# One encoder block on one core: loads of the attention stage a block ahead, the merge of the dilated groups in pinned steps, and gate stores on ScalarE's queue

## The chip, the cores and the metric

The kernel runs on one core of one Trainium2 chip. The metric is the device time of one execution in microseconds (us). The kernel before has a median of 1679.76 us over three runs.

## The reference, cut to what matters

The block takes 1024 tokens of width 1024, all in fp32. One projection of the normalised input gives q, k and v for two token mixers and two gates; both mixers are attention, over different sets of keys.

```python
a = rms_norm(h, g_mix[i])
qa, ka, va, qd, kd, vd, gate_na, gate_dil = jnp.split(a @ w_in[i], split_points, axis=-1)
y_na = merge(neighborhood_attention(heads(qa, 8), heads(ka, 8), heads(va, 8), rpb[i]))
y_dil = merge(dilated_attention(rotary(heads(qd, 12), positions), rotary(heads(kd, 12), positions), heads(vd, 12)))
mixed = sigmoid(gate_na) * (y_na @ w_branch_na[i]) + sigmoid(gate_dil) * (y_dil @ w_branch_dil[i])
h = h + mixed @ w_out[i]
h = h + square(relu(rms_norm(h, g_mlp[i]) @ w_up[i])) @ w_down[i]
h = h + sigmoid(rms_norm(h, g_ple[i]) @ w_ple_gate[i]) * (p[i] @ w_ple_proj[i])
...
def dilated_attention(q, k, v):                # three groups of four heads: (window, dilation)
...
    w = jax.nn.softmax(jnp.stack(lses), axis=0)         # the groups are merged per head slot
    return jnp.einsum('gbhs,gbhsd->bhsd', w, jnp.stack(outs))
```

Neighbourhood attention has eight heads on a 16x64 grid of tokens, with a window of 8x16 and a bias per head.

## The kernel before, in words

**Precision and products.** Every fp32 operand is split into a high and a low part ("hi" and "lo"): ScalarE casts (`split`, L107), VectorE or GpSimd subtracts (L108). A product is three matmuls (hi·hi, lo·hi, hi·lo), a score product two.

**Stages.** The products of the extra input, the v projection and the q, k projection (ten units of seven products, `unit`) come first; q and k go to a DRAM buffer `qk_scr`, v to `v_scr`. Then comes the stage of this change, from about 363 us to 742 us of the span:

- **Gates.** Sixteen pieces of gate weights (`w_in` from number 10) are multiplied with the activations. `gates` (L573 to 588) is a generator; each of its 256 steps is three matmuls of 512 columns. `take` and `prep` (L132 to 144) load a piece (`w_raw`, two buffers, 512 KB), cast it and subtract. The first 24 steps (`FILL_HEAD`) are written ahead of the attention, the others are filled between its tiles, 1.5 steps per dilated tile and 1.35 per neighbourhood tile. A result is copied by ScalarE (L586) and stored to `g_scr` on SyncE's queue (L587), 32 stores.
- **Dilated attention.** Twelve heads (numbers 8 to 19) of eight tiles of 128 queries; heads are served in pairs `pr`. Per head `load_raw` loads q and k, and `operands` (L600 to 613) makes the operands: ScalarE writes `q_st` and `k_st` (L607, L608), VectorE finishes `q_st` (L610), GpSimd makes `k_lo` (L611). Per tile: scores on TensorE, row minimum on VectorE (`nm`, L628), exponent on ScalarE (L630), transposes on TensorE, split, product with v (`av`), and the result added up in `numer`.
- **Neighbourhood attention.** Eight heads (0 to 7), for each four column blocks `cb` of two tiles `qt`. `na_score` loads v (four DMAs) and the bias (L667), which GpSimd negates (L668), and after the exponent VectorE takes a reciprocal (`rs`, L680) and GpSimd normalises the row (`s_sb`, L681). `na_turn` transposes (L691), `na_av` multiplies with v (L713, L714), and VectorE adds up `y_na` (L726).
- **Merge of the dilated groups.** `dil_stats` stores minima and sums of a group, `dil_merge` computes the weights after head 1, and `dil_out(0)`, `dil_out(1)` after heads 3 and 5 scale and add the three groups (L913 to L916; products and sums of 128x1024 on VectorE) into `y_d`.
- **Branches.** Six tiles of `y` are loaded back from `y_scr` (`y_raw`, L972, two buffers), split into `y_op`, and multiplied with the branch weights (`ps_b`); the sigmoids of the gates multiply the result (L989).

**What sets the order.** TensorE's instructions keep the order in which the program writes them (`pe`): scores run three tiles ahead of the transposes (`AHEAD`). On every other engine, SyncE's queue of DMAs among them, a scheduler picks the order from a time simulation of its own, unless an instruction is marked `keep_in_program_order`. Each engine then runs its queue strictly in order, so that an instruction that waits holds up what stands behind it. The DMAs share eight completion semaphores in rotation: one that is to use a semaphore again waits for the earlier DMA on it.

Of the kernel before, what the change touches and what calls it, by code (L numbers as in the profile page):

```python
# [17 lines left out]
P = 128  # L18
S = 1024
# [40 lines left out]
def encoder_kernel(ctx: ExitStack, tc: tile.TileContext, t: dict, out: bass.AP):  # L60
# [69 lines left out]
    flip = [0]  # L130

    def prep(upto):  # L132
        while len(ready) <= min(upto, len(stream) - 1):
            src, i, cols, place = stream[len(ready)]
# [7 lines left out]
            split(wh[:, :cols], wl[:, :cols], raw[:, :cols],  # L142
                  lo_eng=nc.gpsimd if flip[0] % 3 == 0 or 27 <= flip[0] <= 34 else nc.vector)
# [409 lines left out]
    for b in range(2):  # L553
        dma(flat2(act[1][0][b]), a_scr[b])
# [7 lines left out]
    nc.sync.dma_start(band, t["band"])  # L562
    nc.sync.dma_start(blk, t["blk"])
    with ExitStack() as st:
# [7 lines left out]
        def gates():  # L572
            for i in range(16):  # L573
                wh, wl = take(1, 2)[0]
                for half in range(2):
# [11 lines left out]
                    nc.sync.dma_start(g_scr[i, :, half * HALF:(half + 1) * HALF], gs)  # L587
# [4 lines left out]
        def load_raw(h):  # L592

            tag, bufs = ("md", 2) if h < 8 else ("bias", 3)
            q_raw = ap.tile([P, S], F32, name="q_raw", tag=tag, bufs=bufs)
            nc.sync.dma_start(q_raw, qk_scr[h, 0].rearrange("b p n -> (b p) n"))
            kl = aa.tile([P, S], F32R, name="k_lo", tag="kl", bufs=3)
            dma(kl, qk_scr[h, 1].rearrange("b p n -> (b p) n"))
            raws[h] = (q_raw, kl)

        def operands(h):
# [5 lines left out]
            nc.scalar.activation(qs, q_raw, AF.Copy, scale=-0.125)  # L607
# [27 lines left out]
        ready_ops = []  # L635

        def na_tiles(h):

            j, e = h // 2, h % 2
            for pc in range(2):  # L640
                env = {}
                for cb in (2 * pc, 2 * pc + 1):
                    for qt in range(2):
                        yield (lambda cb=cb, qt=qt, env=env: na_score(h, cb, qt, env),
                               lambda cb=cb, qt=qt, env=env: na_turn(cb, qt, env),
                               (lambda cb=cb, env=env: na_av(h, cb, env)) if qt else None)

        na_y, na_bt = {}, {}

        def na_score(h, cb, qt, env):  # L650
# [7 lines left out]
            if cb % 2 == 0 and qt == 0:  # L658
                env["vt"] = aa.tile([P, 2, 4, P], F32R, name="v_t", tag="v_t", bufs=3)
            if qt == 0:  # L660
                for gq in range(4):
                    src = v_scr.rearrange("(g r c) f -> g c r f", c=GW, r=4)[gq, KC0[cb]:KC0[cb] + 32, :,
                                                                            h * P:(h + 1) * P]
                    nc.sync.dma_start(env["vt"][:, cb % 2, gq, :].bitcast(F32), src)
                if cb != 2:
                    bt = ap.tile([P, 2, 384], F32, name="bias", tag="bias", bufs=3)
                    nc.sync.dma_start(bt, t["na_bias"][j, CT[cb], :, e])  # L667
                    nc.gpsimd.tensor_scalar(bt, bt, -1.0, 1.0, op0=ALU.mult, op1=ALU.mult)  # L668
                    na_bt[0] = bt
# [8 lines left out]
            pr, sm = soft(sc, na_bt[0][:, qt, :], 384)  # L678
# [3 lines left out]
            env["pr", cb, qt] = pr  # L682

        def na_turn(cb, qt, env):
# [3 lines left out]
            pr = env.pop(("pr", cb, qt))  # L688
# [5 lines left out]
        def na_av(h, cb, env):  # L694
# [33 lines left out]
            if e == 1 and cb == 3:  # L728
                nc.sync.dma_start(y_scr[j], y)
# [34 lines left out]
        def dil_tiles(g_, pr_):  # L764

            pair = {}
            for e in range(2):
                for half in range(2):
                    env = {}
                    for q in range(4):  # L770
                        yield (lambda e=e, half=half, q=q, env=env: dil_score(g_, pr_, e, half * 4 + q, pair, env),
                               lambda e=e, half=half, q=q, env=env: dil_turn(g_, pr_, e, half * 4 + q, pair, env),
                               (lambda e=e, half=half, env=env: dil_av(g_, pr_, e, half, pair, env)) if q == 3 else None)
# [12 lines left out]
        def dil_score(g_, pr_, e, qi, pair, env):  # L786
# [6 lines left out]
            if qi == 4:  # L793
                ready_ops.append(operands(h + 1 if h < 19 else 0))
                load_raw(h + 2 if h < 18 else h - 18)
# [42 lines left out]
        def dil_av(g_, pr_, e, half, pair, env):  # L838
# [28 lines left out]
            if e == 1 and half == 1:  # L867
                nc.sync.dma_start(n_scr[2 * g_ + pr_], pair["numer"])
# [9 lines left out]
        def dil_merge():  # L878
# [3 lines left out]
            mg, sg, (mx, den, tmp) = small[0:3], small[3:6], small[6:9]  # L882
# [5 lines left out]
            nc.vector.tensor_tensor(tok_view(mx, 1), tok_view(mg[0], 1), nat_view(mg[1], 1), op=ALU.min)  # L888
# [14 lines left out]
        def dil_out(pr_):  # L903
            y = ap.tile([P, S], F32, name="y_d", tag="y")
            for g_ in range(3):
                nm = ap.tile([P, S], F32, name="nm_d", tag="md", bufs=2)
# [573 lines left out]
```

## Time and profile before

| | us |
|---|---|
| median of three runs (lowest, highest) | 1679.76 (1679.47, 1682.87) |
| profiled execution: time, span | 1680.93, 1679.1 |
| TensorE busy, whole span | 1572.6 (94%) |
| VectorE, ScalarE, GpSimd busy, whole span | 1201.1, 712.7, 669.2 |
| stretch 400 to 560 us (dilated attention): TensorE busy | 157.23 of 160 |
| stretch 560 to 740 us (neighbourhood attention): TensorE busy | 150.34 of 180 |

The span is the time between first and last instruction; the time of the execution is 1.8 us longer. TensorE is the busiest engine, and the stages differ: a share over the whole span says nothing of one stage. So the rows below go stage by stage, and within a stage by what TensorE waited for. In the profile, PE is TensorE, DVE VectorE, ACT ScalarE, POOL GpSimd, and SP (SPq) SyncE, which issues the DMAs.

### The profile page before, as it was taken

The numbers are of one execution on the slowest core, as the hardware profiler recorded it, in microseconds if no ns is written. First come the engines' busy times: TensorE is split into PE (matmuls) and PEld (weight loads), VectorE is DVE, ScalarE is ACT, GpSimd is POOL, SyncE is SP. The second block draws the span as 40 slices with busy tenths as digits, with TensorE's granted clock in tenths as the row PEclk, the third lists the DMA queues.
The fourth block names the chain that finished last, engine by engine and source line by source line (L and its number), as shares of the span: only waits on it lengthen the run. The fifth ranks groups of instructions, "written<-read, shape, count | busy, mean of one in ns | idle before, by whom it ended". The sixth has DMA issues, their size and how long they took to land. (4 is left out here: it accounts for less than half of the span.)

```text
span 1679.1 us, 22672 instructions
## 1 busy us (share of the span) xinstructions
PE 1572.6 (94%) x7787; PEld 1313.8 (78%) x7787; DVE 1201.1 (72%) x2020; ACT 712.7 (42%) x1327; POOL 669.2 (40%) x455
## 2 busy tenths in 40 slices
PE   8899999998999988879998899999998999999997
PEld 6899777786888867757786688887877788887886
DVE  6844799735566676745557876767778999999955
ACT  6422222227787765564333433333345333333422
POOL 0233678613122333514303776777742422225100
PEclk9999999998999988989999899999999999999999
DMA  8542455675557668755444244444457545433122
GB/s 293 190 144 105 136 165 158 209 265 213 191 164 208 198 199 257 220 191 171 137 154 147 76 151 160 147 138 145 142 192 283 185 151 166 149 113 125 45 100 70
DMA packets 122355, 279.23 MB, mean 166 GB/s; under 512 B 15392, under 2 KB 39936, under 8 KB 121728
## 3 DMA queue, kind: packets, MB, share of 16 engines
q1 hardware_dynamic: 121088, 275.68, 49.9%
q10 hardware_dynamic: 1152, 2.10, 0.3%
q8 instruction: 62, 1.02, 0.2%
q14 instruction: 53, 0.43, 0.1%
HBM read 186.61 MB, written 91.11 MB: 165 GB/s over the span
## 5 line engine op out<-in xcount | busy, mean ns | idle before, releaser
L107 ACT CAST w_hi<-w_raw 128x1024 fp32r<-128x1024 f32 (+2 forms) x118 | 99.3, 853 | 159.6 <-POOL w_raw L448 55.8
L108 POOL TENSOR_TENSOR w_lo<-w_raw,w_hi 128x1024 fp32r<-128x1024 f32 (+2 forms) x38 | 75.6, 1990 | 209.4 <-ACT w_hi L107 197.4
L108 DVE TENSOR_TENSOR w_lo<-w_raw,w_hi 128x1024 fp32r<-128x1024 f32 (+1 forms) x80 | 97.5, 1225 | 45.6 <-ACT w_hi L107 45.2
L108 DVE TENSOR_TENSOR f_lo<-f_raw,f_hi 128x512 fp32r<-128x512 f32 x80 | 83.0, 1054 | 52.5 <-ACT f_hi L107 51.8
L108 DVE TENSOR_TENSOR pt_l<-tp_p,pt_h 128x384 fp32r<-128x384 f32 (+3 forms) x120 | 64.9, 542 | 27.1 <-ACT pt_h L107 26.6
L107 ACT CAST f_hi<-f_raw 128x512 fp32r<-128x512 f32 x80 | 46.1, 614 | 82.9 <-DMA f_raw<-w_up 79.7
L681 POOL TENSOR_SCALAR s_sb<-s_sb,rs 128x384 f32<-128x384 f32 x64 | 42.1, 662 | 74.1 <-DVE rs L680 54.5
L107 ACT CAST pt_h<-tp_p 128x384 fp32r<-128x384 f32 (+3 forms) x120 | 56.1, 469 | 34.4 <-PE tp_p L691 26.9
L1103 POOL TENSOR_TENSOR u_t<-u_t 128x512 f32<-128x512 f32 x45 | 53.6, 1193 | 38.1 <-ACT u_t L1102 36.9
L611 POOL TENSOR_TENSOR k_lo<-k_lo,k_st 128x1024 fp32r<-128x1024 f32 x12 | 30.2, 2517 | 91.4 <-ACT k_st L608 74.8
L620 PE MATMUL sc<-k_st,q_st 128*128 128x384 f32 (+3 forms) x160 | 54.2, 339 | 8.6 <-DVE q_st L610 4.9
L1102 ACT ACTIVATE u_t<-u_t 128x512 f32<-128x512 f32 x45 | 28.4, 632 | 74.5 <-DVE u_t L1089 74.1
L630 ACT ACTIVATE s_sb<-s_sb,stats 128x256 f32<-128x256 f32 (+2 forms) x96 | 45.0, 469 | 29.5 <-DVE stats L628 28.8
L1266 DVE TENSOR_TENSOR h<-ps_d,h 128x512 f32<-128x512 f32 x84 | 54.2, 677 | 1.3 <-PE ps_d L194 1.2
L630 ACT ACTIVATE s_sb<-s_sb,nm 128x384 f32<-128x384 f32 x64 | 39.5, 618 | 31.8 <-DVE nm L628 30.7
L108 DVE TENSOR_TENSOR f_lo<-f_t,f_hi 128x512 fp32r<-128x512 f32 x32 | 51.3, 1607 | 1.8
L621 PE MATMUL sc<-k_lo,q_st 128*128 128x384 f32 (+3 forms) x160 | 49.8, 311 | 1.6 <-POOL k_lo L611 1.6
L691 PE MATMUL tp_p<-ident,s_sb 128*128 128x128 f32 x192 | 35.0, 295 | 15.0 <-POOL s_sb L681 14.9
L1266 DVE TENSOR_TENSOR sum_t<-ps_d,sum_t 128x512 f32<-128x512 f32 x72 | 46.4, 677 | 1.9 <-PE ps_d L194 1.9
L628 DVE CUSTOM_DVE_ANT_0 s_sb<-sc,bias 128x384 f32<-128x384 f32 x64 | 35.1, 551 | 15.3 <-PE sc L621 13.3
L194 PE MATMUL ps_d<-w_hi,m_op 128*128 128x512 f32 x112 | 43.6, 399 | 2.3 <-DVE m_op L108 2.3
L1228 POOL TENSOR_TENSOR t_raw<-pair,w_raw 128x1024 f32<-128x1024 f32 x6 | 15.5, 2588 | 75.4 <-DMA pair<-w_down 36.3
(474 smaller groups left out, 5814.5 us busy)
## 6 DMA issues: line engine op xcount, KB each, us to landing
f_raw<-w_up SPq DMA_DIRECT2D x32, 512.0 KB
w_raw<-w_in SPq DMA_DIRECT2D x26, 512.0 KB
u_raw<-l_scr SPq DMA_DIRECT2D x25, 512.0 KB
qk_scr<-o SPq DMA_DIRECT2D x96, 128.0 KB
h<-l_scr SPq DMA_DIRECT2D x24, 512.0 KB
l_scr<-u_t SPq DMA_DIRECT2D x42, 256.0 KB
l_scr<-u_s SPq DMA_DIRECT2D x42, 256.0 KB
v_scr<-v_stage SPq DMA_DIRECT2D x20, 512.0 KB
```

Of the source, the lines that this page charges most:

```text
L107: nc.scalar.copy(hi, src)
L108: eng.tensor_tensor(lo, src, hi.bitcast(F32), op=ALU.subtract)
L194: nc.tensor.matmul(ps, sl, mh, start=False, stop=last)
L611: (nc.vector if h < 8 else nc.gpsimd).tensor_tensor(kl, kf, ks.bitcast(F32), op=ALU.subtract)
L620: pe(nc.tensor.matmul(o, qs[:, qsl], kk, start=True, stop=False))
L621: pe(nc.tensor.matmul(o, qs[:, qsl], ll, start=False, stop=True))
L628: nc.vector.tensor_tensor_reduce(s_[:, :n], sc[:, :n], bias, 1.0, 3.0e38, op0=ALU.add, op1=ALU.min, accum_out=nm)
L630: nc.scalar.activation(s_[:, :n], s_[:, :n], AF.Exp, bias=nm, scale=-1.0, accum_out=sm)
L681: nc.gpsimd.tensor_scalar(pr, pr, rs, 1.0, op0=ALU.mult, op1=ALU.mult)
L691: pe(nc.tensor.transpose(tp[:, i * P:(i + 1) * P], pr[:, kb * P:(kb + 1) * P], ident))
L1103: nc.gpsimd.tensor_tensor(c, c, c, op=ALU.mult)
L1266: nc.vector.tensor_tensor(d, ps, d, op=ALU.add)
```

## The change

It has six parts.

1. Gate weights: `load_piece` issues the load of a piece one piece ahead; in the attention stage (`early`) the cast to `w_hi` keeps the program's place on ScalarE, and `w_lo` is made by GpSimd for the pieces up to the twentieth of the stream and by VectorE for those behind (before: every third on GpSimd). `take` looks one piece ahead, not two.
2. Start of the stage: the loads of head 8, of gate piece 10, of the activations, of head 9, and of the two masks are written in this order, and the ScalarE instruction that writes `q_st` keeps the program's place.
3. Gate results are stored on ScalarE's queue.
4. Neighbourhood attention: v and bias are loaded one block (two tiles) ahead, raw q and k of the next head at the second block; its operands are made one tile later than before. Reciprocal and normalisation stand just before the next transposes.
5. The merge: loads at the start of head 1, the computation eight steps (tiles) later. `dil_out` goes group by group: loads, the product five steps later, the sum six steps later, each pinned on VectorE; it starts with head 3 and in the middle of head 5, and ends after the last tile.
6. Stores of `y_na`, `y_d` and `numer` are written two steps later.

```diff
+    def load_piece(n):
+        if n not in loaded and n < len(stream) and stream[n][3] in pools:
+            src, i, cols, place = stream[n]
+            loaded[n] = ring.tile([P, 1024], F32, name="w_raw", tag="w_raw", bufs=2)
+            nc.sync.dma_start(loaded[n][:, :cols], src[i])
...
-            raw = ring.tile([P, 1024], F32, name="w_raw", tag="w_raw", bufs=2)
-            nc.sync.dma_start(raw[:, :cols], src[i])
+            load_piece(n)
+            raw = loaded.pop(n)
...
+            if early[0]:
+                lo_eng = nc.gpsimd if flip[0] <= 20 else nc.vector
+                load_piece(n + 1)
+                tc.keep_in_program_order(nc.scalar.copy(wh[:, :cols], raw[:, :cols]))
+                lo_eng.tensor_tensor(wl[:, :cols], raw[:, :cols], wh[:, :cols].bitcast(F32), op=ALU.subtract)
...
-                    nc.sync.dma_start(g_scr[i, :, half * HALF:(half + 1) * HALF], gs)
+                    nc.scalar.dma_start(g_scr[i, :, half * HALF:(half + 1) * HALF], gs)
...
-            nc.scalar.activation(qs, q_raw, AF.Copy, scale=-0.125)
+            tc.keep_in_program_order(nc.scalar.activation(qs, q_raw, AF.Copy, scale=-0.125))
...
+        def na_loads(h, cb):
...
+            if cb == 2:
+                na_bt[h, 2] = na_bt[h, 1]
+            else:
+                na_bt[h, cb] = ap.tile([P, 2, 384], F32, name="bias", tag="bias", bufs=3)
+                nc.sync.dma_start(na_bt[h, cb], t["na_bias"][h // 2, CT[cb], :, h % 2])
...
-            if cb == 2 and qt == 0 and h < 7:
+            if cb == 1 and qt == 0 and h < 7:
+                load_raw(h + 1)
+            if cb == 2 and qt == 1 and h < 7:
                 ready_ops.append(operands(h + 1))
-                if h < 6:
-                    load_raw(h + 2)
...
+                na_loads(*((h, cb + 1) if cb < 3 else (h + 1, 0)))
...
+            def scaled():
+                dst, a, b = (y, nm, fb) if g_ == 0 else (tok_view(fb, g_), nat_view(nm, g_), tok_view(fb, g_))
+                tc.keep_in_program_order(nc.vector.tensor_tensor(dst, a, b, op=ALU.mult))
...
+                if g_ < 2:
+                    dil_out(pr_, g_ + 1, y)
                 else:
-                    nc.vector.tensor_tensor(tok_view(fb, g_), nat_view(nm, g_), tok_view(fb, g_), op=ALU.mult)
-                    nc.vector.tensor_tensor(y, y, fb, op=ALU.add)
-            nc.sync.dma_start(y_scr[4 + pr_], y)
+                    later(2, lambda: nc.sync.dma_start(y_scr[4 + pr_], y))
+
+            later(5, scaled)
+            later(6, added)
...
         load_raw(8)
-        ready_ops.append(operands(8))
+        load_piece(10)
+        for b in range(2):
+            dma(flat2(act[1][0][b]), a_scr[b])
         load_raw(9)
+        nc.sync.dma_start(band, t["band"])
+        nc.sync.dma_start(blk, t["blk"])
+        ready_ops.append(operands(8))
+        early[0] = True
         for _ in range(FILL_HEAD):
             next(fill)
...
             if h == 1:
-                after[len(tiles)] = dil_merge
+                after.setdefault(len(tiles) - 8, []).append(dil_merge)
             elif h in (3, 5):
-                after[len(tiles)] = lambda pr_=h // 2 - 1: dil_out(pr_)
+                after.setdefault(len(tiles) - (8 if h == 3 else 3), []).append(lambda pr_=h // 2 - 1: dil_out(pr_))
```

TensorE's order stays as it was but for two products of the branches (`ps_b`), which no longer stand ahead of the last `av`. Three places of the order in the other queues follow.

**ScalarE where the stage begins.** `p1` is the last copy of the q, k projection, `w_hi` the cast of a gate piece, `q_st` and `k_st` the operands of head 8 (and 9). Before:

```order
L107 CAST w_hi_3441<-w_raw_3439 128x1024
L107 CAST w_hi_3447<-w_raw_3445 128x1024
L532 COPY p1_3361<-ps_q_3348 128x512
L107 CAST w_hi_3453<-w_raw_3451 128x1024
L107 CAST w_hi_3515<-w_raw_3513 128x1024
L586 COPY g_st_3482<-ps_g_3457 128x512
L586 COPY g_st_3510<-ps_g_3485 128x512
L107 CAST w_hi_3690<-w_raw_3688 128x1024
L586 COPY g_st_3544<-ps_g_3519 128x512
L607 ACTIVATE q_st_3429<-q_raw_3425 128x1024
L608 CAST k_st_3430<-k_lo_3427 128x1024
```

The same place now:

```order
L546 COPY p1_3361<-ps_q_3348 128x512
L616 ACTIVATE q_st_3435<-q_raw_3421 128x1024
L617 CAST k_st_3436<-k_lo_3423 128x1024
L154 CAST w_hi_3441<-w_raw_3425 128x1024
L154 CAST w_hi_3447<-w_raw_3443 128x1024
L596 COPY g_st_3478<-ps_g_3453 128x512
L597 DMA g_scr_93<-g_st_3478 128x512
L596 COPY g_st_3506<-ps_g_3481 128x512
L597 DMA g_scr_93<-g_st_3506 128x512
L154 CAST w_hi_3509<-w_raw_3449 128x1024
```

The operands of head 8 stood behind the first three gate results and stand ahead of the first gate weights' cast now; on GpSimd `k_lo` of head 8 likewise stands ahead of the `w_lo` of the first two pieces.

**SyncE's queue at the same time**, from the last stores of the q, k projection (`qk_scr`) on. Before:

```order
L138 DMA w_raw<-w_in 128x1024
L752 DMA v_t<-v_scr 64x256
L275 DMA k_lo<-qk_scr 128x1024
L275 DMA qk_scr<-o_3295 64x1024 x3
L275 DMA qk_scr<-o_3294 64x1024 x4
L275 DMA qk_scr<-o_3295 64x1024
L138 DMA w_raw<-w_in 128x1024 x2
L596 DMA q_raw<-qk_scr 128x1024 x2
L587 DMA g_scr<-g_st 128x512 x2
```

Now:

```order
L778 DMA v_t<-v_scr 64x256
L289 DMA k_lo<-qk_scr 128x1024
L289 DMA qk_scr<-o_3295 64x1024 x3
L289 DMA qk_scr<-o_3294 64x1024 x4
L289 DMA qk_scr<-o_3295 64x1024
L605 DMA q_raw<-qk_scr 128x1024 x4
L137 DMA w_raw<-w_in 128x1024 x3
L605 DMA q_raw<-qk_scr 128x1024
```

The first `q_raw` still stands behind the eight stores; three loads of gate weights that stood ahead of it here, and one further up, are behind it now.

**SyncE's queue at the end of the stage**, where `y` goes to DRAM and is read back. Before:

```order
L917 DMA y_scr<-y_d 128x1024
L667 DMA bias<-na_bias 128x768
L982 DMA gt<-g_scr 128x2x512 x3
L138 DMA w_raw<-w_br 128x768
L972 DMA y_raw<-y_scr 128x1024
L982 DMA gt<-g_scr 128x2x512
L587 DMA g_scr<-g_st 128x512
L982 DMA gt<-g_scr 128x2x512
L972 DMA y_raw<-y_scr 128x1024 x2
L729 DMA y_scr<-y_na 128x1024
```

Now:

```order
L958 DMA y_scr<-y_d 128x1024
L1037 DMA gt<-g_scr 128x2x512
L755 DMA y_scr<-y_na 128x1024
L1027 DMA y_raw<-y_scr 128x1024
L137 DMA w_raw<-w_br 128x768
L1027 DMA y_raw<-y_scr 128x1024 x5
```

Three of the six loads stood ahead of the last `y_na` store, and all six stand behind it now.

## Rows read from the trace of the kernel before

**Rows 1.** Windows by stage: us; PE, PEld, DVE, ACT, POOL busy; clock; DMA share; GB/s.

```profile
360.00:379.50 19.50, 19.39 (x86) 15.74 (x84) 5.67 (x7) 4.12 (x5) 0.00 (x0) 1.00 1.03 375
379.50:388.00 8.50, 1.65 (x5) 1.15 (x5) 4.41 (x5) 5.92 (x8) 6.47 (x3) 0.73 1.02 381
388.00:400.00 12.00, 12.00 (x57) 9.98 (x58) 5.25 (x18) 7.12 (x20) 1.68 (x2) 0.77 0.43 160
400.00:560.00 160.00, 157.23 (x935) 131.69 (x934) 97.42 (x281) 121.65 (x307) 35.03 (x17) 1.00 0.58 181
560.00:740.00 180.00, 150.34 (x837) 127.01 (x836) 122.61 (x319) 113.50 (x246) 69.26 (x87) 0.91 0.73 221
```

**Rows 2.** Waits of PE, 560 to 742 us: total us, times, longest.

```profile
PE tp_p L691 <- POOL s_sb L681: 14.9, 9, 3.1
PE av L713 <- ACT pt_h L107: 4.6, 2, 3.6
PE av L713 <- ACT s_sb L630: 3.8, 2, 2.1
PE sc L620 <- DVE nm L628: 3.3, 2, 2.0
```

**Rows 3.** Waits of POOL, the same stretch.

```profile
POOL bias L668 <- DMA bias<-na_bias: 33.4, 13, 7.3
```

**Rows 4.** Timeline of PE, 362 to 387 us: start, us, what; in brackets the wait before.

```profile
362.91 0.39 PE L584 MATMUL ps_g<-act00h,w_hi 128*128 128x512 f32 x1
...
379.01 0.39 PE L584 MATMUL ps_g<-act01h,w_lo 128*128 128x512 f32 x1
384.25 0.50 PE L620 MATMUL sc<-k_st,q_st 128*128 128x192 f32 x1 [4.86 <-DVE q_st L610]
386.37 0.53 PE L621 MATMUL sc<-k_lo,q_st 128*128 128x192 f32 x1 [1.62 <-POOL k_lo L611]
```

**Rows 5.** Timeline of ACT, 381 to 383 us.

```profile
381.80 1.06 ACT L607 ACTIVATE q_st<-q_raw 128x1024 fp32r<-128x1024 f32 x1 [1.71 <-DMA q_raw<-qk_scr]
382.76 1.03 ACT L608 CAST k_st<-k_lo 128x1024 fp32r<-128x1024 f32 x1
```

**Rows 6.** Timeline of POOL, 379 to 390 us.

```profile
379.69 2.34 POOL L108 TENSOR_TENSOR w_lo<-w_raw,w_hi 128x1024 fp32r<-128x1024 f32 x1 [20.98 <-ACT w_hi L107]
383.87 5.76 POOL L611 TENSOR_TENSOR k_lo<-k_lo,k_st 128x1024 fp32r<-128x1024 f32 x2 [1.84 <-ACT k_st L608]
```

**Rows 7.** Timeline of SyncE's queue, 365 to 376 us: a row is the time to issue.

```profile
365.16 8.18 SPq L275 DMA_DIRECT2D qk_scr<-o  x8
373.44 1.33 SPq L138 DMA_DIRECT2D w_raw<-w_in  x2
374.82 0.91 SPq L596 DMA_DIRECT2D q_raw<-qk_scr  x2
```

**Rows 8.** Timelines of POOL and then of DVE, 572 to 714 us.

```profile
572.98 0.83 POOL L668 TENSOR_SCALAR bias<-bias 128x768 f32<-128x768 f32 x1 [3.41 <-DMA bias<-na_bias]
698.46 2.04 POOL L668 TENSOR_SCALAR bias<-bias 128x768 f32<-128x768 f32 x1 [3.48 <-DMA bias<-na_bias]
...
697.81 2.02 DVE L915 TENSOR_TENSOR fb_d<-nm_d,fb_d 128x1024 f32<-128x1024 f32 x1 [1.34 <-DMA fb_d<-f_scr]
708.93 3.31 DVE L915 TENSOR_TENSOR fb_d<-nm_d,fb_d 128x1024 f32<-128x1024 f32 x1
```

**Rows 9.** Timelines at the end of the stage: SyncE's queue, ACT, DVE.

```profile
735.84 0.32 SPq L972 DMA_DIRECT2D y_raw<-y_scr  x1
...
740.43 1.05 ACT L107 CAST y_op<-y_raw 128x1024 fp32r<-128x1024 f32 x1 [1.80 <-DMA y_raw<-y_scr]
...
742.76 0.75 DVE L726 TENSOR_TENSOR y_na<-av,fold 64x256 f32<-64x256 f32 x2
759.25 1.23 DVE L108 TENSOR_TENSOR y_op<-y_raw,y_op 128x1024 fp32r<-128x1024 f32 x1 [2.73 <-ACT y_op L107]
```

**Rows 10.** Waits of SyncE's queue, 400 to 742 us.

```profile
SPq L587 <- ACT g_st L586: 56.6, 16, 9.4
```

More of the change, by code (lines that the diff above doesn't have):

```diff
@@ L573, in gates @@
             for i in range(16):
-                wh, wl = take(1, 2)[0]
+                wh, wl = take(1, 1)[0]
                 for half in range(2):
@@ L592, in load_raw @@
         def load_raw(h):
-            tag, bufs = ("md", 2) if h < 8 else ("bias", 3)
-            q_raw = ap.tile([P, S], F32, name="q_raw", tag=tag, bufs=bufs)
+            q_raw = ap.tile([P, S], F32, name="q_raw", tag="bias", bufs=3)
             nc.sync.dma_start(q_raw, qk_scr[h, 0].rearrange("b p n -> (b p) n"))
@@ L635, in encoder_kernel, with later @@
         ready_ops = []
+        after, now = {}, [0]
+        def later(n, f):
+            after.setdefault(now[0] + n, []).append(f)
         def na_tiles(h):
@@ L728, in na_av @@
             if e == 1 and cb == 3:
-                nc.sync.dma_start(y_scr[j], y)
+                later(2, lambda: nc.sync.dma_start(y_scr[j], y))
         env_head = {}
@@ L933, in encoder_kernel @@
         load_raw(8)
+        load_piece(10)
+        for b in range(2):
+            dma(flat2(act[1][0][b]), a_scr[b])
+        load_raw(9)
+        nc.sync.dma_start(band, t["band"])
+        nc.sync.dma_start(blk, t["blk"])
         ready_ops.append(operands(8))
-        load_raw(9)
+        early[0] = True
         for _ in range(FILL_HEAD):
             next(fill)
-        tiles, after = [], {}
+        tiles = []
         for g_ in range(3):
@@ L941, in encoder_kernel @@
                 tiles += [(x, FILL_DIL) for x in dil_tiles(g_, pr_)]
-            after[len(tiles) + 2] = lambda g_=g_: dil_stats(g_)
+            after.setdefault(len(tiles) + 2, []).append(lambda g_=g_: dil_stats(g_))
         for h in range(8):
@@ L945, in encoder_kernel @@
             if h == 1:
-                after[len(tiles)] = dil_merge
+                after.setdefault(len(tiles) - 8, []).append(dil_merge)
             elif h in (3, 5):
-                after[len(tiles)] = lambda pr_=h // 2 - 1: dil_out(pr_)
-        late = None
-        for i in range(-AHEAD, len(tiles) + 1):
+                after.setdefault(len(tiles) - (8 if h == 3 else 3), []).append(lambda pr_=h // 2 - 1: dil_out(pr_))
+        late, i = None, -AHEAD
+        while i <= len(tiles) or any(n >= i for n in after):
+            if 0 <= i + AHEAD - 1 < len(tiles) and tiles[i + AHEAD - 1][0][3]:
+                tiles[i + AHEAD - 1][0][3]()
             if 0 <= i < len(tiles):
@@ L956, in encoder_kernel @@
                 tiles[i + AHEAD][0][0]()
+            now[0] = i
             if late:
@@ L959, in encoder_kernel @@
             late = tiles[i][0][2] if 0 <= i < len(tiles) else None
-            if i in after:
-                after[i]()
+            for f in after.pop(i, ()):
+                f()
             pay(1.0)
+            i += 1
+        early[0] = False
         for _ in fill:
```

83 lines of the change are left out of this document (46 added, 37 removed).

## The prediction

> **What bounds the kernel now.** I read the windows by stage first [rows 1]. Up to 379.5 us and in the dilated attention (400 to 560) TensorE is busy without a break worth having: 157.23 us of 160, at the full granted clock. There no other queue can give time, only take it. Two stretches are different. Between 379.5 and 388 us TensorE works 1.65 us of 8.5, and in the neighbourhood attention (560 to 740) 150.34 of 180, with a mean clock of 0.91.
>
> The waits come next. In the neighbourhood stage TensorE's largest is for the normalised rows from GpSimd, 14.9 us in nine waits [rows 2]; GpSimd itself stood 33.4 us for bias tiles, up to 7.3 us at a time [rows 3]. Since GpSimd runs its queue in order, a late bias holds up the normalisation behind it. The other waits [rows 2] are for ScalarE (4.6 and 3.8) and for the row minimum from VectorE (3.3). At the start the timelines of TensorE, ScalarE, GpSimd and SyncE's queue [rows 4 to 7] show what the first score waited for: `q_raw`, which arrived at 381.8 us [rows 5], 7.0 us after its issue at 374.82 [rows 7], while the 24 gate steps (362.91 to 379.4) filled the time [rows 4].
>
> **The change, part by part.** The sum is made against the profiled execution, 1680.93 us, which is 1.17 us above the median of the runs.
>
> *Start of the stage: +14 us.* Before, the gate steps covered the way of `q_raw`. Now ScalarE's first work after the projection is `q_st`, and the first two casts of gate weights stand behind it; on GpSimd `k_lo` stands ahead of the first `w_lo`. So the gate steps wait for the load that they used to cover. When does it land? Its place behind the eight `qk_scr` stores (8.18 us to issue [rows 7]) is the same; four loads of gate weights of 512 KB are no longer ahead of it, 2.1 MB, which at 375 GB/s [rows 1] take 5.6 us: 381.8 - 5.6 = 376.2 us. From there the chain goes by measured steps [rows 5, 6]: `k_st` starts 0.96 later and takes 1.03 (378.2), `k_lo` takes 5.76/2 = 2.88 (381.1), `w_lo` 2.34 (383.4). The third matmul of the first gate step needs that `w_lo`. TensorE, done with the projection at 362.9, stands about 20 us. Then the 24 steps take 16.5 us as before and end at 399.9; the operands of head 8 are there by then. The scores ran from 386.4 us before [rows 4]: 399.9 - 386.4 = +13.5, rounded up to 14. Bounds: if the queue in front of it drains earlier and `q_raw` lands at 371, +9; if the loads taken away save nothing, `w_lo` ends at 389 and it is +19. The clock fell after the old wait too (0.77 in the 12 us behind it [rows 1], 12 x 0.23 = 2.8 us lost); I take the same loss behind the new one, and up to 3 us more for the upper end.
>
> *Dilated attention: 0.* Twenty stores of gate results move to ScalarE, which is busy 121.65 of 160 us [rows 1]; 38 us are free for 20 issues, and an issue on SyncE's queue takes under half a us (0.46 for a `q_raw` [rows 7]). Bounds 0 and what the rival on ScalarE's queue says below. SyncE gets rid of waits of 56.6 us for the gate copies [rows 10], which held back loads behind them; in this stage nothing waits for those.
>
> The Trainium skill, "DMA: Bandwidth & Descriptors", section "Issuing engines are not separate DMA queues", states that DMAs started by ScalarE run on the same 16 engines and that only issue time is saved. By it this part would be worth nothing anywhere. The rows say more: the queue of SyncE is in order, and its 56.6 us of waiting [rows 10] stood ahead of bias loads. I count that gain once, in the next term.
>
> *Neighbourhood attention: -25 us.* What could be won? Idle time is 180 - 150.34 = 29.7 us. The clock of 0.91 [rows 1] lies between two levels, full and half, so about 18% of the stage, 32 us, ran at half, which loses at most 16 us. The ceiling is 46. Bias and v now come a block (5.6 us at 180/64 = 2.8 per tile) earlier; 33.4 us in 13 waits [rows 3] is 2.6 each, so nearly all of them should be covered, and with them the 14.9 us of `tp_p` [rows 2]. The merge no longer parks VectorE on a load (1.34 us ahead of L915 [rows 8]), worth about 1 of the 3.3 us of `nm` [rows 2]. That is 16 of 29.7 us idle; the clock falls behind waits, so I take the same share of its loss, 16/29.7 x 16 = 8.6. Together 25. The waits for ScalarE stay. What is late next is VectorE: `q_st` and `k_lo` of the next head, six products and four sums of the merge (2 to 3.3 us a product [rows 8]), and `w_lo` of six gate pieces now made there. VectorE has 180 - 122.61 = 57 us free [rows 1], so this costs in bursts only. Bounds: -9, if only a third of `tp_p` and its clock go (5 + 3) and the 1 us of `nm`, and -40, if nearly all goes.
>
> GpSimd's instructions stretch beside large VectorE ones: the negation of a bias takes 0.83 us alone and 2.04 beside the product at L915 [rows 8]. The Trainium skill, "GPSIMD Engine Reference", section "1. Specifications", states that GpSimd shares its SBUF interfaces with VectorE, with contention when a VectorE instruction has two SBUF inputs. By that rule more `w_lo` on GpSimd in the dilated stage and the pinned merge products beside its normalisations would cost up to 1.2 us a meeting, six meetings 7 us. I leave it in the range, since the same products stood there before.
>
> *End of the stage: +4 us.* The second merge ends after the last tile, so two VectorE instructions of it (2 to 3.3 us and, by a 128x1024 difference, 1.23 [rows 8, 9]) stand among the last splits, and all six `y_raw` loads wait for the last `y_na` (744.3 us before [rows 9]). One load takes 740.43 - 735.84 = 4.6 us, a cast 1.05 and a subtraction 1.23 [rows 9]; two buffers make three rounds of 6.9 us, the last `y_op` at 744.3 + 20.7 = 765, 4.5 us later than 759.25 + 1.23 = 760.5. TensorE's work between covers some of it, the merge adds some. Bounds 0 and 8.
>
> *Sum:* 1680.93 + 14 + 0 - 25 + 4 = 1673.9, and 1.17 less for the median: **1673 us**. With 9 to 19, -18 to -32 and 0 to 8 its own range is 1664 to 1682.
>
> **The rivals.**
>
> *The start costs little.* If `q_raw` lands by some 365 us, the head start pays for itself: the gates begin early and the scores find everything ready, so the start costs 3 us in place of 14: 1662. For it: two loads of weights no longer stand in front of the stores either. Against it: the DMA engines are full at 375 GB/s [rows 1], and the eight stores stand ahead.
>
> *Everything in the neighbourhood stage closes:* -40 in place of -25, 1658. For it: the waits for ScalarE follow the others. Against it: VectorE's bursts remain.
>
> *The loads don't come earlier in fact,* so the change does not do there what it says. SyncE's queue is still in order; v and bias now stand behind `q_raw`, `k_lo` and a gate piece whose buffer waits for VectorE's `w_lo`. Then the stage gives 9 in place of 25: 1689.
>
> *ScalarE waits behind its own stores.* A store needs a completion semaphore from the rotation, and ScalarE stands until the earlier DMA on it, perhaps one that SyncE has not yet been able to issue, is done. In the dilated stage ScalarE has 38 us to spare for 20 stores, so this decides from 1.9 us each. At 3 us each (a load here takes 4.6 [rows 9]) it costs 20 x 1.1 = 22: 1695, slower than before. For it: exponents and splits stand behind the store, and TensorE has no slack there [rows 1]. Against it: loads are issued well ahead in that stage.
>
> **How the numbers follow.** Chances: forecast 0.40, cheap start 0.16, everything closes 0.08, late loads 0.20, ScalarE's stores 0.16. A measurement of this kernel tells about 0.2% from no change, 3.4 us, so "same" is 1676.4 to 1683.1. The forecast with its own spread gives 0.28 faster, 0.08 same, 0.04 slower; the two cheap cases 0.24 faster; the late loads 0.04 same and 0.16 slower; ScalarE's stores 0.02 same and 0.14 slower. That makes 0.52, 0.14 and 0.34. The range goes from 1658 to 1692; it leaves out the lower half of the case at 1658 and parts of the two slow ones, under 0.2 together.
>
> **What would show it.** In the new profile TensorE should stand near 20 us between the projection and the first gate step, waiting for `w_lo` from GpSimd, then work through 24 gate steps before any score. Right for the neighbourhood stage: GpSimd's waits for the bias near zero, TensorE's for `tp_p` under 3 us, busy above 160 us of 180 or the stage some 25 us shorter, clock above 0.95. At the end all `y_raw` follow the last `y_na`. Wrong would be a first gate step before 370 us, bias waits above 15 us, or ScalarE waiting for DMAs ahead of exponents in the dilated stage. The stages outside should keep their lengths within 2 us.

## The result, and the profile after

The change makes the kernel slower: a median of 1695.48 us (1693.16 to 1699.41, four runs) against 1681.32 us for the kernel before on the same chip, a ratio of 1.0086 with a 95% interval of 1.006 to 1.0113. That is above the range of the prediction (1658 to 1692).

The profiled execution took 1693.16 us, 12.2 more than the one before. Three landmarks of TensorE's and VectorE's timelines divide this: the first score of the neighbourhood attention, the last `av` product, the last `y_op` subtraction.

| us | before | after | difference | predicted |
|---|---|---|---|---|
| start of the span to the first neighbourhood score | 555.4 | 571.1 | +15.7 | +14 |
| from there to the last `av` (neighbourhood stage) | 184.7 | 175.1 | -9.6 | -25 |
| from there to the last `y_op` (end of the stage) | 19.1 | 25.4 | +6.3 | +4 |

They sum to +12.4. The windows by stage after, moved along with the stages (columns as in [rows 1]):

```profile
361.50:381.50 20.00, 1.23 (x3) 0.50 (x2) 1.91 (x2) 3.88 (x4) 4.76 (x3) 0.59 0.85 289
381.50:401.00 19.50, 19.12 (x76) 15.44 (x76) 0.80 (x5) 3.46 (x5) 4.71 (x3) 0.89 0.30 100
401.00:560.00 159.00, 154.01 (x899) 129.05 (x900) 89.27 (x260) 118.32 (x297) 47.11 (x19) 0.98 0.58 179
560.00:740.00 180.00, 153.44 (x900) 130.27 (x899) 132.13 (x350) 117.64 (x269) 65.86 (x89) 0.95 0.74 226
740.00:757.00 17.00, 5.68 (x32) 4.18 (x32) 5.44 (x8) 8.51 (x11) 1.80 (x1) 0.82 0.67 230
```

TensorE now idles 18.8 of the first 20 us and works through the gate steps after that. For the neighbourhood stage the windows between its two landmarks, before and after, tell more:

```profile
555.44:740.18 184.74, 154.96 (x860) 130.67 (x859) 126.96 (x332) 116.42 (x253) 69.85 (x88) 0.91 0.72 219
571.13:746.22 175.09, 146.25 (x857) 123.94 (x856) 128.55 (x334) 112.11 (x250) 65.03 (x88) 0.95 0.74 226
```

TensorE's idle time in the stage is 29.8 us before and 28.8 after. Nearly all of the 9.6 us is busy time: the same matmuls, but for three of the branches, took 146.25 us in place of 154.96, at a mean granted clock of 0.95 in place of 0.91. The start, on PE, ACT and POOL (timelines; compare [rows 4 to 6]):

```profile
377.66 0.80 PE L594 MATMUL ps_g<-act00h,w_hi 128*128 128x512 f32 x1 [16.16 <-ACT w_hi L154]
...
381.56 0.80 PE L594 MATMUL ps_g<-act00h,w_lo 128*128 128x512 f32 x1 [2.67 <-POOL w_lo L155]
```

```profile
374.67 1.06 ACT L616 ACTIVATE q_st<-q_raw 128x1024 fp32r<-128x1024 f32 x1 [17.98 <-DMA q_raw<-qk_scr]
375.64 1.03 ACT L617 CAST k_st<-k_lo 128x1024 fp32r<-128x1024 f32 x1
376.57 1.99 ACT L154 CAST w_hi<-w_raw 128x1024 fp32r<-128x1024 f32 x2
```

```profile
376.74 2.46 POOL L620 TENSOR_TENSOR k_lo<-k_lo,k_st 128x1024 fp32r<-128x1024 f32 x1 [27.69 <-ACT k_st L617]
379.17 4.65 POOL L155 TENSOR_TENSOR w_lo<-w_raw,w_hi 128x1024 fp32r<-128x1024 f32 x2
```

This is the chain of the prediction, link by link: ScalarE stands 18 us for `q_raw`, the gate's casts and `w_lo` follow, and TensorE's third matmul starts at 381.56.

The waits of PE (576 to 757 us) and the wait of POOL for the bias in the same stretch, against [rows 2, 3]:

```profile
PE tp_p L717 <- POOL s_sb L708: 12.7, 8, 3.8
PE ps_b L206 <- ACT y_op L107: 9.0, 1, 9.0
PE av L740 <- DVE pt_l L108: 8.6, 7, 3.9
PE av L739 <- ACT pt_h L107: 4.5, 3, 2.4
...
POOL bias L692 <- DMA bias<-na_bias: 24.3, 11, 4.3
```

The wait for normalised rows is nearly what it was (14.9), GpSimd still stands 24.3 us for biases (33.4), and two waits are new or larger: `pt_l` from VectorE (1.8 us before) and `y_op` at the end. The end, on SyncE's queue:

```profile
746.70 0.33 SPq L958 DMA_DIRECT2D y_scr<-y_d  x1
...
747.97 0.36 SPq L755 DMA_DIRECT2D y_scr<-y_na  x1
750.76 0.33 SPq L1027 DMA_DIRECT2D y_raw<-y_scr  x1
...
754.33 12.67 SPq L1027 DMA_DIRECT2D y_raw<-y_scr  x5
```

The merge's `y_d` is stored only at 746.70, and all six loads follow the last `y_na`.

### The profile page after: what moved, and what is told of

Same layout as the page of the kernel before. It is cut to its first block, busy times and chain, and to the rows that moved or that the text cites. A ratio compares the mean times of both kernels' runs of the same rounds, so it can differ in the third digit from the quotient of the medians.

```text
span 1691.3 us, 22551 instructions
## 1 busy us (share of the span) xinstructions
PE 1566.1 (93%) x7787; PEld 1308.3 (77%) x7787; DVE 1191.8 (70%) x2016; ACT 707.4 (42%) x1325; POOL 677.9 (40%) x459
## 5 line engine op out<-in xcount | busy, mean ns | idle before, releaser
L107 ACT CAST w_hi<-w_raw 128x512 fp32r<-128x512 f32 (+2 forms) x101 | 81.7, 822 | 135.7 <-POOL w_raw L462 55.5
L108 POOL TENSOR_TENSOR w_lo<-w_raw,w_hi 128x512 fp32r<-128x512 f32 (+2 forms) x32 | 62.4, 1952 | 150.2 <-ACT w_hi L107 93.6
L108 DVE TENSOR_TENSOR w_lo<-w_raw,w_hi 128x1024 fp32r<-128x1024 f32 (+1 forms) x69 | 82.5, 1202 | 33.3 <-ACT w_hi L107 33.0
L708 POOL TENSOR_SCALAR s_sb<-s_sb,rs 128x384 f32<-128x384 f32 x64 | 41.8, 658 | 71.4 <-DVE rs L707 56.6
L637 DVE CUSTOM_DVE_ANT_0 s_sb<-sc,band 128x256 f32<-128x256 f32 (+1 forms) x64 | 26.4, 413 | 41.7 <-PE sc L630 41.1
L206 PE MATMUL ps_b<-y_op,w_hi 128*128 128x512 f32 x96 | 38.8, 413 | 12.2 <-ACT y_op L107 9.9
L639 ACT ACTIVATE s_sb<-s_sb,nm 128x384 f32<-128x384 f32 x64 | 39.4, 616 | 22.7 <-DVE nm L637 21.8
L717 PE MATMUL tp_p<-ident,s_sb 128*128 128x128 f32 x192 | 33.6, 286 | 15.5 <-POOL s_sb L708 12.7
```

The source lines that it names most:

```text
L107: nc.scalar.copy(hi, src)
L108: eng.tensor_tensor(lo, src, hi.bitcast(F32), op=ALU.subtract)
L206: nc.tensor.matmul(ps, sh, mh, start=first, stop=False)
L637: nc.vector.tensor_tensor_reduce(s_[:, :n], sc[:, :n], bias, 1.0, 3.0e38, op0=ALU.add, op1=ALU.min, accum_out=nm)
L639: nc.scalar.activation(s_[:, :n], s_[:, :n], AF.Exp, bias=nm, scale=-1.0, accum_out=sm)
L708: nc.gpsimd.tensor_scalar(pr, pr, rs, 1.0, op0=ALU.mult, op1=ALU.mult)
```

## The experiments

Each kernel ran on one chip beside the kernel before. The ratio is to that kernel (medians 1678.2 to 1679.5 us in these comparisons); the stage columns come from one profiled execution each, with the landmarks of the first table. That execution is not always a typical one: it lies 2.0 to 6.6 us above the median in runs 12, 9, 2 and 14 (most in run 14) and 4.2 below it in run 15, so a difference of a few us between two stage columns shows little.

| run | median us | ratio, 95% | to first score | stage | end |
|---|---|---|---|---|---|
| 1 operands late | 1676.38 | 0.9988 [0.9972, 1.0003] | 550.9 | 177.6 | 25.8 |
| 2 = 1, gate stores on SyncE | 1686.24 | 1.0049 [1.003, 1.0068] | 551.7 | 188.8 | 26.0 |
| 3 = 1, no merge | 1662.38 | 0.9902 [0.987, 0.9934] | 555.9 | 169.4 | 12.2 |
| 4 = 3, q_raw in own buffers | 1656.21 | 0.9873 [0.9845, 0.9901] | 552.0 | 174.9 | 9.7 |
| 5 = 1, negation pinned at its block | 1674.67 | 0.9977 [0.9967, 0.9988] | 551.1 | 177.5 | 26.2 |
| 6 = 1, negation pinned a tile earlier | 1667.18 | 0.9944 [0.9927, 0.996] | 551.9 | 167.2 | 25.4 |
| 7 = 1, merge earlier | 1669.47 | 0.9952 [0.9938, 0.9967] | 550.2 | 180.5 | 19.8 |
| 8 before, gate stores on ScalarE | 1676.73 | 0.9983 [0.9967, 0.9999] | 553.8 | 180.7 | 22.0 |
| 9 = 6 and 7 | 1662.99 | 0.9912 [0.9886, 0.9938] | 549.4 | 174.3 | 19.6 |
| 10 = 9, w_lo on GpSimd | 1671.86 | 0.9956 [0.9939, 0.9974] | 550.3 | 181.2 | 19.5 |
| 11 = 1, loads at own block | 1667.66 | 0.9939 [0.9918, 0.996] | 548.3 | 169.1 | 26.6 |
| 12 = 1, bias at own block | 1677.57 | 0.999 [0.9969, 1.0011] | 549.2 | 179.8 | 24.6 |
| 13 = 1, v at own block | 1674.87 | 0.9981 [0.9964, 0.9998] | 550.3 | 179.4 | 25.0 |
| 14 = 11 and 7 | 1673.16 | 0.9968 [0.9946, 0.999] | 550.9 | 185.3 | 19.4 |
| 15 = 1, old merge | 1685.91 | 1.0044 [1.0028, 1.0061] | 550.9 | 197.5 | 11.4 |
| 16 = 15 and 6 | 1683.85 | 1.003 [1.0015, 1.0046] | 552.0 | 200.1 | 11.6 |

**Run 1: the start.**

```diff
-        ready_ops.append(operands(8))
         early[0] = True
-        for _ in range(FILL_HEAD):
+        for n_ in range(FILL_HEAD):
+            if n_ == 20:
+                ready_ops.append(operands(8))
             next(fill)
```

> The changed kernel with one edit: the operands of head 8 are written after 20 of the 24 head steps of the gates, not ahead of them. Theory: of the changed kernel's loss, about 16 us arise at the start, because the casts of the first gate weights stand behind q_st. Then the first gate step starts within 2 us of the end of the projection, the wait falls from 19 us to 5 to 7 us ahead of the first score, and the time falls by 11 to 15 us to about 1682 us, level with the kernel before. Rival: the gates would have waited for their weights or the memory anyway; then a wait of over 12 us remains and the time falls by under 5 us.

It fell by 19.1 us to 1676.38 by medians (17.3 us when each is taken against the kernel before beside it), more than the 11 to 15 expected. The gates run straight on, and the first score waits 2.64 + 1.78 us (PE):

```profile
381.19 0.33 PE L629 MATMUL sc<-k_st,q_st 128*128 128x192 f32 x1 [2.64 <-DVE q_st L619]
383.30 0.53 PE L630 MATMUL sc<-k_lo,q_st 128*128 128x192 f32 x1 [1.78 <-POOL k_lo L620]
```

The first neighbourhood score comes 20.2 us earlier than in the changed kernel. The place of `operands(8)` alone makes the loss at the start, and one move of a line turns a slower kernel into one level with the kernel before.

**Runs 2 and 8: whose queue stores the gates.** Run 2 is run 1 with `nc.sync.dma_start(g_scr...)` again; run 8 is the kernel before with `nc.scalar.dma_start(g_scr...)`.

> As the run with the operands late, and gate results stored on SyncE's queue again. If the stores on ScalarE's queue help, because SyncE no longer stands for the gate copies (56.6 us of waits before), bias waits of GpSimd rise above the changed kernel's 24 us and the time rises by 3 to 8 us against that run. Rival one: nothing (within 3 us), if loads were held back by other things. Rival two: ScalarE lost time behind its own stores; then the time falls by 3 us or more.

> The kernel before with one edit: the gate results are stored on ScalarE's queue. Theory: SyncE's waits for the gate copies (56.6 us) go, the neighbourhood stage shortens by 4 to 10 us, the time falls to 1670 to 1676 us. Rival one: in this kernel the loads do not stand behind those waits when it matters; within 3 us. Rival two: ScalarE stands behind its own stores; slower by 3 us or more.

Run 2 rose by 9.9 us, 11.2 of it in the neighbourhood stage. Waits of SyncE's queue (400 to 740 us) and of PE (552 to 720) in run 2:

```profile
SPq L597 <- ACT g_st L596: 34.0, 11, 5.2
```

```profile
PE tp_p L717 <- POOL s_sb L708: 22.3, 10, 5.6
```

With the stores back, SyncE stands 34.0 us for gate copies, GpSimd's waits for the bias go from 39.2 to 45.3 us (552 to 742 us) and TensorE's for normalised rows from 14.5 (run 1, same stretch) to 22.3 us. But the one is not shown to be the reason of the other: 31.8 of the 34.0 us lie in the dilated stage, which lost nothing, and 2.2 in the stage that grew by 11.2. In the kernel before, the opposite edit took 4.0 us off the stage and gave 2.9 back at its end; its time fell by 2.6 us, as rival one said, with an interval that ends just under no change. So the store's place comes with 10 us among the other parts and with little alone, and how it acts stays open. ScalarE paid nothing: a store is 0.33 us on its queue, with no wait ahead of it (changed kernel, ACT):

```profile
428.02 0.33 ACTq L597 DMA_DIRECT2D g_scr<-g_st  x1
```

**Runs 3 and 4: without the merge.** Both leave out the merge; run 4 also has `tag, bufs = ("md", 2) if h < 8 else ("bias", 3)` for `q_raw`.

```diff
-            if h == 1:
-                after.setdefault(len(tiles) - 8, []).append(dil_merge)
...
-                after.setdefault(len(tiles) - (8 if h == 3 else 3), []).append(lambda pr_=h // 2 - 1: dil_out(pr_))
+                after.setdefault(len(tiles) - (8 if h == 3 else 3), []).append(lambda pr_=h // 2 - 1: dil_copy(pr_))
...
+        def dil_copy(pr_):
+            y = ap.tile([P, S], F32, name="y_d", tag="y")
+            nc.sync.dma_start(y, n_scr[pr_])
+            later(2, lambda: nc.sync.dma_start(y_scr[4 + pr_], y))
```

> As the run with the operands late, and the merge of the dilated groups is left out: minima and sums are not merged, and instead of the weighted sum of three groups the first group's numerator is copied to y through SBUF. Theory one (SyncE's queue and the ring of three buffers that q_raw now shares with the bias keep the loads late): GpSimd's waits for the bias stay above 12 us, and the neighbourhood stage shortens by at most 6 us, the end of the stage by 2 to 4. Theory two (VectorE's bursts from the pinned products and sums are what is left): the neighbourhood stage shortens by 10 us or more and TensorE's waits for pt_l fall from 8.6 to under 3 us.

> As the run without the merge (the same part is left out), and q_raw of the neighbourhood heads has two buffers of its own, those that the merge leaves free, so that the three bias buffers hold only biases. Theory one: SyncE's waits for the row minimum and q_st ahead of q_raw and bias loads go, GpSimd's waits for the bias fall under 8 us, and the time falls by another 4 to 8 us. Theory two: bias waits may fall, but the time stays within 3 us.

Run 3 fell by 14.0 us, 8.2 in the stage and 13.6 at its end, with 5.0 lost ahead of the stage. The end is more than was expected, the stage lies between the two theories, and the waits for `pt_l` stayed (7.9 to 6.5 us), against theory two. Bias waits stayed at 34.1 us, as theory one said. Run 4's median is another 6.2 us lower, but the stage in its profile is 5.5 us longer, and bias waits rose (43.4 us from 560 to 740): theory one's reason does not hold, and where the 6.2 us come from stays open.

**Runs 5 and 6: the place of the negation.** Both pin the normalisation on GpSimd as well.

```diff
-                    nc.gpsimd.tensor_scalar(bt, bt, -1.0, 1.0, op0=ALU.mult, op1=ALU.mult)
+                    tc.keep_in_program_order(nc.gpsimd.tensor_scalar(bt, bt, -1.0, 1.0, op0=ALU.mult, op1=ALU.mult))
```

Run 6 writes it at the second tile of the block before: `else: negate(*((h, cb + 1) if cb < 3 else (h + 1, 0)))`.

> As the run with the operands late; the negation of the bias and the normalisation keep the program's order on GpSimd, so that a bias is negated just before its first tile, two tiles after its load was issued, and no longer as soon as the scheduler thinks it has landed. In the run before this one a negated bias lay unused for 2 to 8 us. Theory: it is the place of the negation in GpSimd's queue, not the load, that holds up the normalisations; then GpSimd's waits for the bias fall from 39 us to under 8, TensorE's waits for tp_p from 13.9 to under 5 us, and the time falls by 5 to 12 us. Rival: the load itself is late (SyncE's queue); then the waits move to VectorE's row minimum, and the time stays within 3 us or rises.

> As the last run, with the negation pinned one tile earlier, at the second tile of the block before. If the row minimum in the last run has to wait for a fresh negation, this one is faster than it by 2 us or more; if the landing of the load matters (one tile is 2.8 us, a bias takes 3.5 to 4 us from issue to negation), it is slower, with 10 to 20 us of GpSimd's waits for the bias. Theory: within 3 us of the last run.

In both, GpSimd's 39.2 us of waits for the bias are gone altogether. The time tells them apart: run 5 gained 1.7 us only, with more waiting for normalised rows (22.8 us, not under 5), run 6 gained 9.2 (the stage is 10.4 shorter). Run 5 came out as its rival said, though not for the rival's reason: no load is late there. One place shows how it works. Run 1, POOL and then DVE:

```profile
620.29 0.58 POOL L708 TENSOR_SCALAR s_sb<-s_sb,rs 128x384 f32<-128x384 f32 x1
625.84 0.83 POOL L692 TENSOR_SCALAR bias<-bias 128x768 f32<-128x768 f32 x1 [4.96 <-DMA bias<-na_bias]
626.65 1.71 POOL L708 TENSOR_SCALAR s_sb<-s_sb,rs 128x384 f32<-128x384 f32 x3
...
632.83 0.56 DVE L637 CUSTOM_DVE_ANT_0 s_sb<-sc,bias 128x384 f32<-128x384 f32 x1 [0.60 <-PE sc L630]
```

GpSimd stands 4.96 us for a bias whose first reader, counted by tiles, comes at 632.83, 6.2 us after the negation; three normalisations stand behind it, and TensorE waits 3.17 us for the first. In run 6 the same place (POOL) reads:

```profile
623.03 0.59 POOL L714 TENSOR_SCALAR s_sb<-s_sb,rs 128x384 f32<-128x384 f32 x1 [5.17 <-DVE rs L713]
623.58 0.83 POOL L683 TENSOR_SCALAR bias<-bias 128x768 f32<-128x768 f32 x1
624.39 0.59 POOL L714 TENSOR_SCALAR s_sb<-s_sb,rs 128x384 f32<-128x384 f32 x1
```

No load is waited for, and TensorE's wait there is 1.35 us. The expectation that both places are alike was wrong. The pins use up the time that a bias lay ready: in run 1 no first reader comes sooner than 1.2 us after its negation, in run 5 13 of 24 come within 0.1 us, in run 6 nine. VectorE waits for a fresh negation about as long in both (7.2 us in run 5, 7.7 in run 6), so that is not the difference; why the earlier place is so much better was not found.

**Runs 7, 9 and 10: the end of the stage, and the two together.**

```diff
-                after.setdefault(len(tiles) - (8 if h == 3 else 3), []).append(lambda pr_=h // 2 - 1: dil_out(pr_))
+                after.setdefault(len(tiles) - (12 if h == 3 else 8), []).append(lambda pr_=h // 2 - 1: dil_out(pr_))
```

> As the run with the operands late; the groups of the two merges start 4 and 5 tiles earlier, so that the second ends before the last tiles and two y_raw loads stand ahead of the last y_na store again. Theory: the end of the stage lost 5 us (TensorE stood 9.5 us for y_op) because all six y_raw loads wait for the last store; that wait falls under 5 us and the time falls by 3 to 6 us. Rival: the merge only meets other tiles, the neighbourhood stage pays it back, and the time stays within 2 us.

> The three edits together: operands late, negation pinned one tile ahead of its block (normalisation pinned too), merge groups earlier. Theory: the two last act in different places (GpSimd's queue in the stage, loads of y at its end) and add up: 9.2 and 6.9 us off the run with the operands late, so about 1660 us, 18 to 21 us under the kernel before. Rival: they share a cause (the merge's products hold up VectorE ahead of the normalisations in either case); then it stays at 1665 to 1669.

> As the last run, and w_lo of all pieces prepared during the attention is made by GpSimd. Theory: TensorE's waits for pt_l (8 to 10 us, 1.8 in the kernel before) come from long VectorE instructions ahead of pt_l, w_lo's 1.2 us among them; they fall by 2 to 4 us, and the time by 1 to 4. Rival: GpSimd, at 2.3 us a piece, now delays normalisations by as much; the time stays or rises by up to 4 us.

Run 7 fell by 6.9 us. The end went from 25.8 to 19.8 us, close to the 19.1 of the kernel before; TensorE's wait for `y_op` from 10.7 to 7.0 (expected: under 5). Run 9, at 1662.99 us, beats both kernels, by 16.2 us the one before. It is 4.2 us under run 6, not 6.9: the end gains 5.8, and the stage is 7.1 longer than in run 6, in a profiled execution that lies 3.2 us above its median, so each expectation held in part. Run 10 (`lo_eng = nc.gpsimd` throughout) rose by 8.9 us, more than its rival said, though TensorE's waits for `pt_l` fell only from 9.7 to 7.7.

**Runs 11 to 14: the loads a block ahead.** Run 11 replaces the call by `na_loads(h, cb)`; run 12 moves only the bias back, run 13 only v; run 14 is run 11 with the merge earlier.

> As the run with the operands late, but bias and v are loaded at their own block as in the kernel before, not one block ahead. The prediction gave the early loads nearly all of its 25 us. Theory now: GpSimd stands 3.5 to 5 us behind each bias load wherever it is, since the scheduler moves the negation with the load; then bias waits stay at 30 to 45 us and the time stays within 4 us of 1676. Rival: the early loads do give time; then it rises by 5 us or more.

> As the run with the operands late; the bias is loaded at its own block, v stays a block ahead. Theory: the early bias costs the time, because its negation goes ahead with it on GpSimd; then this run takes back most of the 9 us, to 1667 to 1670 us. Rival: the early v costs it (SyncE's queue, three buffers); then this run stays at 1674 to 1678.

> As the run with the operands late; v is loaded at its own block, the bias stays a block ahead. Theory: within 2 us of 1676. Rival (early v costs it): 1667 to 1670.

> Operands late, bias and v at their own block, merge groups earlier. If the stage and its end are separate, the two gains add up: 8.7 and 6.9 us off 1676, about 1661 us. If not, it stays above 1665.

Bias waits in run 11 are 45.8 us, and the time is 8.7 us lower than run 1, which neither its theory nor its rival said. The edit moves the loads far less than the program says: from the issue of a bias to the first row minimum that reads it pass 9.9 us (median of the 24 biases) in run 11 and 11.1 in run 1: a load is issued when SyncE's queue comes to it, not at the tile where the program writes it. In run 4 the loads do come earlier (15.2 us, 10.5 in run 3), and its stage is no shorter than run 3's. So early loads give no time here. But neither half explains why undoing them gains: run 12 and run 13 stayed at 1677.57 and 1674.87, and run 14 is 12 us above the sum expected, with a stage of 185.3 us in an execution 6.6 us above its median. I read this as the scheduler's order: each edit re-sorts all queues but TensorE's, and that moves the stage by several us either way. That is an argument; which queue does it was not found.

**Runs 15 and 16: the merge in pinned steps.** They put the old `dil_merge` and `dil_out` back in their old places, run 16 with the negation of run 6.

> As the run with the operands late, with the merge as in the kernel before: weights after head 1, both sums in one piece after heads 3 and 5, in the scheduler's order. Theory: the pinned products and sums stand ahead of pt_l on VectorE whenever they come; then TensorE's waits for pt_l fall under 4 us, the end of the stage gets its two early y loads back (TensorE's wait for y_op under 6 us, as in the run with the merge earlier), and the time falls by 6 to 12 us to 1664 to 1670. Rival: pinning is worth what it was meant for; the end gains its 5 us, the stage loses as much or more to waits for the row minimum, and the time is 1674 or more.

> As the last run, with the negation pinned one tile ahead of its block. Theory: 4 to 9 us under the last run. Rival: the old merge's waits for its loads on VectorE (3.6 us in the kernel before) come back and eat it; within 3 us of the last run.

The rival was right in its outcome. Run 15 rose by 9.5 us: the end shortened to 11.4 us, and the stage grew by 19.9. TensorE's waits there are for normalised rows (19.7 us) and `pt_h` (8.2) more than for the row minimum (2.7), and those for `pt_l` stayed (9.1), against the theory. Waits of DVE (552 to 742 us), and the largest gap of PE, in run 15:

```profile
DVE fb_d L945 <- DMA fb_d<-f_scr: 9.4, 3, 4.2
DVE fb_d L945 <- DMA v_t<-v_scr: 2.3, 1, 2.3
```

```profile
630.72 0.90 PE L717 MATMUL tp_p<-ident,s_sb 128*128 128x128 f32 x3 [7.06 <-POOL s_sb L708]
```

VectorE stands for the merge's loads with row minima and reciprocals behind it. Pinned steps avoid these waits, as the change meant them to. They are longer here than they were in the kernel before, where VectorE stood 5.2 us for the merge's loads in the same stretch. Run 16 is 2.1 us under run 15, as its rival said.

## Why the prediction was wrong

*The sum.* The median is 22.7 us above the forecast before rounding. The neighbourhood stage makes 15.4 of them, the start 1.7 and the end 2.3. Another 3.5 come from the step to the median: it was taken to lie 1.17 us below the profiled execution and lies 2.3 above it.

*Start, +14: right.* `q_raw` was worked out to land at 376.2 us and ScalarE took it at 374.67; `w_lo` was to end at 383.4, and the matmul that needs it started at 381.56. By the row minima the first dilated tile comes 12.5 us later than before. Run 1 takes the whole term away by one moved line.

*Dilated attention, 0: nearly right; ScalarE's stores as a rival: refuted.* Over the first eight tiles the lag behind the kernel before grows from 12.5 to 16.2 us, which makes the 15.7 of the table: TensorE waits 1.4 us each for `pt_l` and for exponents, and its granted clock is 0.82 from 401 to 420 us. After that the stage kept its length. A store is 0.33 us on ScalarE's queue and waits for nothing; the rival whose time, 1695, came nearest to the measured one was not the reason for it.

*Neighbourhood attention, -25: this is the step that failed.* It measured -9.6. The step said that bias and v come 5.6 us earlier, that nearly all of GpSimd's 33.4 us of bias waits are therefore covered, and with them TensorE's 14.9 us of `tp_p`. All three links fell.

The loads did not come earlier. I counted from the issue of each bias to the first row minimum that reads it: a median of 12.3 us in the kernel before and 11.2 in the changed one. One such pair of each, SyncE's queue and DVE, before and then after:

```profile
657.97 0.58 SPq L667 DMA_DIRECT2D bias<-na_bias  x1
669.59 0.56 DVE L628 CUSTOM_DVE_ANT_0 s_sb<-sc,bias 128x384 f32<-128x384 f32 x1 [0.96 <-PE sc L621]
```

```profile
634.88 0.35 SPq L675 DMA_DIRECT2D bias<-na_bias  x1
646.10 0.55 DVE L637 CUSTOM_DVE_ANT_0 s_sb<-sc,bias 128x384 f32<-128x384 f32 x1
```

In the kernel before, which writes a load at its own tile, SyncE's queue already issued it that early. The rival of late loads (1689) said just this, and a stage that gives 9; its reason, that they stand behind `q_raw` and a gate piece, is not shown.

The waits were not covered: 24.3 us after and 39.2 in run 1, because the scheduler, where nothing pins it, places the negation right behind the load, mostly 3.2 to 5 us after its issue in either kernel.

And the waits were not the price. A bias lay ready for a median of 6 us before its first reader in either kernel, and of TensorE's 14.9 us for normalised rows 7.9 stood behind a negation that waited for its load (6.9 of 12.7 after); most of the others stood behind VectorE's reciprocal. Run 5 has no such waits and gains 1.7 us, run 11 has 45.8 and is 8.7 faster. The row said who stood, not that anyone needed it.

The gain that did come has another make-up than the sum. Of the 16 us of idle time 0.9 went. The 8.6 us of clock came nearly whole (8.7 us of busy time, 0.7 of it the three matmuls that moved), without the waits from which they were derived; that is luck, and run 1, with the same edits in the stage, has 27.3 us idle and 150.3 busy at a clock of 0.93. That the measured -9.6 lies at the lower bound of -9 is luck too, since the bound was added up from waits.

*Within that step, two terms can't be sized from the runs.* The merge off VectorE's way was put at about 1 us; run 15 shows 19.9 us in the stage, with 14.4 given back at its end, but against the new order, with waits for the merge's loads (11.7 us) that the kernel before did not have at that length (5.2). The store on ScalarE's queue was counted inside the early loads, by the reading that SyncE's 56.6 us stood ahead of bias loads; only 8.8 of them lie in the neighbourhood stage. Run 2 shows 11.2 us there, run 8 4.0. These effects do not add up to 9.6 us, and what else in the change costs the stage time is not found. VectorE's bursts, said to cost little, showed as waits for `pt_l`, from 1.8 to 8.6 us.

*End of the stage, +4: right in mechanism, measured +6.3.* All six loads behind the last `y_na` store; run 7 moves the merge and takes 6.0 us back.

The Trainium skill's rule on issuing engines ("DMA: Bandwidth & Descriptors", section "Issuing engines are not separate DMA queues") would have made the stores worth their issue time only. Runs 2 and 8 measure 9.9 and 2.6 us, more than that in run 2. Whether it is saved by SyncE no longer standing for the data, or by the order that the scheduler made of each edit, these runs do not show.

## What to carry to other kernels

A wait in the profile is worth time only if what is queued behind it is late for its reader: find the reader, and measure the slack, before a load is moved ahead. Then check in the new profile that the load's issue has moved against its reader: where a scheduler orders the queue, a place in the program is not a place in the queue. When one instruction is pinned in an order that a scheduler fills, look at what stands behind it on the same engine; here the pinned `q_st` put the cover behind the load it used to cover. Stores issued by the engine that makes the result cost that engine 0.33 us each here and spared the loading queue its waits for them; what that was worth in time, 2.6 or 9.9 us, hung on the order around it.

## What was not expected of the hardware

GpSimd's negation of a bias took 0.83 us at most places and 1.36 and 1.20 at 662 and 669.6 us in the changed kernel. Over its stage, negations and normalisations took 6.0 us more than at 0.83 and 0.58 us each, against 11.1 us in the kernel before, so the meetings with large VectorE instructions cost less and not more. Order alone moved this stage far: with the same instructions on TensorE, its length went from 167.2 to 200.1 us over the runs that leave nothing out, more than any single wait in their tables.
